# A hybrid encoder block on one core: the last gate half in seven products, and q and k computed among three gate halves

## The chip, the cores and the metric

The kernel runs on one core of one Trainium2 chip. The metric is the device time of one execution in microseconds; of several runs the median is taken. The core's engines work side by side and each takes its own instructions in order: TensorE (PE: matmuls, with PEld for its weight loads), VectorE (DVE), ScalarE (ACT), GpSimd (POOL) and SyncE (SP). DMAs are issued by SP, ACT and POOL and carried by 16 DMA engines.

## What is computed

One layer over 256 tokens of width 2048, all in float32:

```python
xn = rms_norm(x, norm_pre_w[l])
z = xn @ w_in[l]
u_lru, g_lru, q, k, v, g_attn, m_lru, m_attn = jnp.split(z, split_at, axis=-1)
u = centred_depthwise_conv(u_lru, conv_w[l], conv_b[l])
h = (rg_lru(u, ..., False) + rg_lru(u, ..., True))
y_a = h.astype(x.dtype) * jax.nn.silu(g_lru)
q = partial_rope(q.reshape(bsz, s, N_HEADS, HEAD_DIM), cos, sin)
k = partial_rope(k.reshape(bsz, s, N_KV_HEADS, HEAD_DIM), cos, sin)
y_b = windowed_gqa(q, k, v, attn_sink[l]) * jax.nn.silu(g_attn)
merged = (jax.nn.sigmoid(m_lru) * (y_a @ w_proj_a[l])
          + jax.nn.sigmoid(m_attn) * (y_b @ w_proj_b[l]))
x = x + rms_norm(merged @ w_out[l], norm_post_w[l])
```

There are 16 heads of 128 columns in four groups, each group with its own k and v. The rotation (`partial_rope`) touches the first 32 columns of each head. The gates m_lru and m_attn have 2048 columns each.

## The kernel before

**Number format.** Every float32 operand of a matmul is split into a high part (a cast, on ACT) and a low part (the difference, on DVE), and a product is taken as three matmuls: high by high, high by low, low by high (`mm3`, L221). Activations are split once, weights as they arrive.

**Steps.** The program is a list of steps, written out by hand as words in `START`, `MERGE` and `OUT` (L55 to L66). One step is 1 MB of weights, in two halves. A letter names the product, a number its column block, the digit behind the dot its part along the contraction:

- `u`, `w`: the LRU's input; `g`, `h`: its silu gate and that of attention; `v`, `k`, `q`: attention; `p`, `b`: the two projections; `a`: the gate m_attn; `o`: the output product.
- Steps of g, h, w, k and q ("blk", `add_pair`, L227) hold weights as the stationary operand and take 8 matmuls of 512 and 8 of 256 columns a half. Steps of v, p, a, b and o ("quad", `add_rows`, L257) hold activations and take 12 matmuls of 512 columns a half.
- `Lm1.0` and the like ("part", class `Seven`, L338): half a gate (1024 columns) by Strassen's scheme, seven products m1 to m7 in place of eight, each in two parts of 12 matmuls. L and M are the two halves of m_lru, A the second half of m_attn, O half of the output product. The first half of m_attn is eight plain quads, a0 and a1. The sums of weights that m3 to m7 need are made by accumulating DMAs from POOL into "x" and "y" cells (`load`, L185). The sums of x are made once (`x_sums`, L327), kept in DRAM and loaded again for each gate half (`x_sum`, L333).

**Time in the program.** A half of a blk or quad and a whole part are one half step ("tick", L157). The loop at L1095 goes through the steps. At each half it issues the loads of the steps three to five ahead (`fetch`, L199), then the work that is due at this half step, then the cast for four halves ahead and the subtraction for three halves ahead (`split`, L207), then the matmuls. Work is put at a half step with `at`, or a number of half steps from now with `soon` (L160, L172); an engine's queue is filled in this order. Raw weights have a ring of three buffers; everything else lives in 45 units of 4 KB a partition. What does not fit is written to DRAM by `park` (L782) and fetched by `back` (L789), both on SP's queue, on which the raw loads are too.

**Order around the change.** Before, the gate halves L and M are woven into the steps of g, h, w and k. Then come q0, p0, q1, p1, q2, p2, q3, p3, then a0 and a1 woven with A, then b with the rest of A and the start of O, then the output.

**Attention.** `add_heads` (L804) takes a group's two column pairs from PSUM: `evac` (L809) scales them and `rotate` (L817) turns each pair's first 32 rows with operations on 32 partitions by 512, then splits them. `heads` (L916) puts the four heads of a group behind its q: the first head's scores five half steps later (`HEAD0`), the next ones every four (`STRIDE`). A head (L846) takes scores at its half step b, the masked maximum on DVE at b + 1, the exponentials on ACT at b + 2, the scale by the sum (L878) at b + 4, the transposes on PE (`flip`, L880) at b + 5, the split of the transposed at b + 6; a pair of heads is multiplied with v at b + 10. `yb_parts` (L911) splits the gated result for b. `gates`' sigmoids are taken by `gate_evac` (plain, L749) or `gate_sum` (seven products, L758); `gated_out` (L745) parks those of m_lru.

Of the kernel before, what the change touches and what calls it, by code (L numbers as in the profile page):

```python
# [15 lines left out]
F32 = mybir.dt.float32  # L16
# [13 lines left out]
UNITS = 45  # L30
DECAY = 12
SPIN = 10
HEAD0 = 5
STRIDE = 4
FIRST = 8
ROWS = 10
U0, GL0, Q0, K0, V0, GA0, ML0, MA0 = 0, 2048, 4096, 6144, 6656, 7168, 9216, 11264

# [13 lines left out]

MERGE = """q0.0 q0.1 q0.2 q0.3 p0.0 p0.1 p0.2 p0.3 q1.0 q1.1 q1.2 q1.3 p1.0 p1.1 p1.2 p1.3  # L55
    q2.0 q2.1 q2.2 q2.3 p2.0 p2.1 p2.2 p2.3 q3.0 q3.1 q3.2 q3.3 p3.0 p3.1 p3.2 p3.3
    a0.0 a0.1 Am1.0 a0.2 Am1.1 a0.3 Am2.0 a1.0 Am2.1 a1.1 Am5.0 a1.2 Am5.1 a1.3 b0.0 Am3.0 b0.1 Am3.1 b0.2 Am6.0
    b0.3 Am6.1 b1.0 b1.1 Am7.0 b1.2 Am7.1 b1.3 b2.0 Am4.0 b2.1 Am4.1 b2.2 b2.3 b3.0 Om1.0 b3.1 Om5.0 b3.2 b3.3""".split()
OUT = """o2.0 o2.1 Om1.1 o2.2 Om5.1 Om2.0 o2.3 Om3.0 Om6.0 Om3.1 o3.0 Om6.1 Om2.1 o3.1 Om7.0 Om7.1 Om4.0 Om4.1
    o3.2 o3.3""".split()  # L60

START = """u0.0 u0.1 u0.2 u0.3 v0.0 v0.1 v0.2 v0.3 g0.0 g0.1 h0.0 h0.1 w4.0 w4.1 g2.0 g2.1 h2.0 h2.1 w6.0 w6.1 g4.0 g4.1
    Lm1.0 h4.0 h4.1 Lm1.1 w8.0 Lm2.0 w8.1 Lm2.1 g6.0 Lm5.0 g6.1 h6.0 Lm5.1 h6.1 Lm3.0 w10.0 Lm3.1 w10.1 Lm6.0 g8.0
    g8.1 Lm6.1 h8.0 Lm7.0 h8.1 Lm7.1 w12.0 Lm4.0 w12.1 g10.0 Lm4.1 g10.1 Mm1.0 h10.0 Mm1.1 h10.1 Mm2.0 w14.0 w14.1
    Mm2.1 g12.0 Mm5.0 g12.1 Mm5.1 h12.0 Mm3.0 h12.1 g14.0 Mm3.1 g14.1 Mm6.0 h14.0 Mm6.1 h14.1 Mm7.0 k0.0 k0.1 Mm7.1
    k2.0 Mm4.0 k2.1 Mm4.1""".split()  # L66
XSUM = (18, 22, 26, 30, 34, 38, 42, 46)
LRU = (-4, 0, 2, 2, 2, 2, 2, 4)
QUADS = {"u": ("w_in", U0), "v": ("w_in", V0), "p": ("w_proj_a", 0), "a": ("w_in", MA0),
         "b": ("w_proj_b", 0), "o": ("w_out", 0)}  # L70
PAIRS = {"g": GL0, "h": GA0, "w": U0, "k": K0, "q": Q0}
SEVENS = {"L": ("w_in", ML0 + 1024), "M": ("w_in", ML0), "A": ("w_in", MA0 + 1024), "O": ("w_out", 0)}


PV_NORM = 0
# [38 lines left out]
def body(ctx, tc, x, xT, wall, wlru, pvec, npost, ident_d, mask_d, rope_d, out):  # L114
# [9 lines left out]
    def unit(name, dt=F32, shape=(P, 4, S)):  # L124
        return units.tile(list(shape), dt, tag="u", name=name)
# [7 lines left out]
    def half_unit(name, tag, dt=F32, bufs=2):  # L133
        return small.tile([P, 2, S], dt, tag=tag, name=name, bufs=bufs)
# [10 lines left out]
    def parts_of(h, l, src):  # L145
        nc.scalar.copy(h, src)  # L146
        soon(lambda: nc.vector.tensor_tensor(l, src, h.bitcast(F32), ALU.subtract))
# [24 lines left out]
    def soon(fn, d=1):  # L172
        at(now[0] + d, fn)
# [396 lines left out]
    def scaled(dst, ps, then=lambda: None, rows=True):  # L570
        def scale(src):
            nc.vector.tensor_tensor(dst, src, rbc.unsqueeze(1).to_broadcast([P, 2, S]), ALU.mult)
            then()

        def total():
            nc.vector.tensor_tensor(dst, ps[:, :, 0], dst, ALU.add)
            if rows:
                scale(dst)
            else:
                then()  # L580

# [161 lines left out]
        return gates[c]  # L743

    def gated_out(gates, c, t):  # L745
        if t == 1 and gates is tm:
            soon(lambda: park("tm", tm, c), 5)

    def gate_evac(gates, c):  # L749
        def done(t, ps):  # L750
# [7 lines left out]
    def gate_sum(gates, first=2):  # L758

        def done(t, c, ps, other, sign):  # L760
            to = gate_unit(gates, first + c)[:, t]

            def gate(src):
                nc.scalar.activation(to, src, AF.Sigmoid, scale=rtok[:, t:t + 1])
                gated_out(gates, first + c, t)

            if other is None:
                gate(ps)
            else:
                combine(to, ps, other, sign)  # L770
                soon(lambda: gate(to))
        return done

    Seven("L", xs, None, gate_sum(tm))
    Seven("M", xs, None, gate_sum(tm, 0))
    Seven("A", xs, None, gate_sum(sm))
    for n in range(8):
        behind(XSUM[n], lambda n=n: x_sums(n))
# [17 lines left out]

    def load_tables():
        t = unit("table")
        table.update(mask=t[:, 0:2], rope=t[0:ROT, 2:4])
        nc.sync.dma_start(table["mask"], mask_d)  # L800
        nc.sync.dma_start(table["rope"], rope_d)


    def add_heads(name, then):  # L804


        v = {}

        def evac(n):  # L809
            def done(ps):  # L810
                v[n] = half_unit(f"{name}f{n}", "uu")
                scaled(v[n], ps, rows=name == "k")
                for d in range(4):
                    soon(lambda d=d: rotate(n, d), d + 2)
            return done

        def rotate(n, d):  # L817
            t = v[n]
            r = t[0:ROT]
            if d == 0:  # L820
                v["s"] = small.tile([ROT, 2, S], F32, tag="upad", name=f"{name}s{n}", bufs=2)
                nc.vector.stream_shuffle(v["s"], r, swap)
                nc.vector.tensor_tensor(r, r, table["rope"][:, 0].unsqueeze(1).to_broadcast([ROT, 2, S]), ALU.mult)
            elif d == 1:
                s = v["s"]
                nc.vector.tensor_tensor(s, s, table["rope"][:, 1].unsqueeze(1).to_broadcast([ROT, 2, S]), ALU.mult)
                nc.vector.tensor_tensor(r, r, s, ALU.add)
            elif d == 2:
                if n == 0:
                    v["h"], v["l"] = unit(f"{name}h", F32R), unit(f"{name}l", F32R)  # L830
                parts_of(v["h"][:, n:n + 2], v["l"][:, n:n + 2], t)
            elif n == 2:
                then(v["h"], v["l"])
                v.clear()
# [11 lines left out]
    def head(hd, qh, ql, b, both):  # L846

        g, j = hd // 4, hd % 4
        sk = pv[:, PV_SINK + hd:PV_SINK + hd + 1]
# [48 lines left out]
        def gate_out():  # L898
            y = sga[g][:, j - 1:j + 1]
            nc.vector.tensor_tensor(y, both["o"], y, ALU.mult)  # L900
            both.clear()
            if j == 3 and g < 3:
# [13 lines left out]
    def heads(g):  # L916
        def then(h, l):
            b = now[0] + HEAD0
            soon(lambda: back("sga", sga, g, (P, 4, S)), HEAD0 + 4)
            for j in range(4):  # L920
                if j % 2 == 0:
                    both = {}
                head(4 * g + j, h, l, b + STRIDE * j, both)
        return then


    def add_pa(c):
# [44 lines left out]
        return tick  # L972

    seven = Seven("O", ms, msum, lambda *a: o_sum(*a))
    heads_k = add_heads("k", lambda h, l: kv.update(kh=h, kl=l))

    def add_q(c):
        pair = add_heads(f"q{c}", heads(c))
        for n in (0, 2):
            pair(n)  # L980

# [11 lines left out]
        "a": lambda: add_rows(f"ma{c}_", xs, gate_evac(sm, c)),  # L993
# [195 lines left out]
```

## Time and profile before

| | |
|---|---|
| median of 3 runs | 889.14 us (889.12 to 889.55) |
| the profiled execution | 889.43 us, of which span 887.1 us |
| granted TensorE clock | 0.998 |
| moved by DMA | 235.13 MB, mean 265 GB/s |

The span runs from the first to the last instruction in the profile of one execution; the rest of that execution's time lies around it. The profile's page gives busy shares by engine, the chain of work that ended last (followed back from the last instruction to whatever released it), and groups of instructions with their line, shapes, total and mean. Idle time of an engine that is not on the chain costs nothing by itself.

### The profile page before, as it was taken

To read this page: it belongs to the slowest core of one execution; us is meant where nothing else is said; L and a number is where in the kernel's file an instruction comes from. 1 tells how busy PE (TensorE), PEld (TensorE's weight loads), DVE (VectorE), ACT (ScalarE), POOL (GpSimd) and SP (SyncE) were. 2 spreads that over 40 slices of the span, in tenths; PEclk is the share of its full clock that TensorE was granted. 3 is DMA by queue.
4 is the path that set the end of the run, shared out by engine and by line. 5 is a ranking of instruction groups with operands and counts; after the bars stand their busy time and mean duration, and the time that the engine had idled before them with its cause. 6 is when DMAs were issued, how large, how long until landed. Compare 5 with 4: busy or idle time off the path is not lost.

```text
span 887.1 us, 12275 instructions
## 1 busy us (share of the span) xinstructions
PE 877.8 (99%) x4566; PEld 753.3 (85%) x4566; DVE 713.3 (80%) x974; ACT 610.4 (69%) x885; POOL 58.6 (7%) x88
## 2 busy tenths in 40 slices
PE   9999999999999999999999999999999999999996
PEld 8888888888888888888888888888888888888885
DVE  6999999798988788989987678586667776687776
ACT  7689687878788787989654556356687564555654
POOL 0000000011001011100000000000101100000200
PEclk9999999999999999999999999999999999999999
DMA  9757699999968999974957456558999997899962
GB/s 331 270 191 250 197 366 235 375 312 301 313 235 240 312 313 313 308 243 145 350 190 276 175 206 217 188 192 321 249 318 329 306 300 244 284 325 377 236 177 96
DMA packets 51419, 235.13 MB, mean 265 GB/s; under 512 B 5376, under 2 KB 10240, under 8 KB 35104
## 3 DMA queue, kind: packets, MB, share of 16 engines
q1 hardware_dynamic: 41568, 200.03, 61.2%
q0 software_dynamic: 9216, 33.56, 19.4%
q10 hardware_dynamic: 576, 0.76, 0.3%
q8 instruction: 36, 0.59, 0.3%
q14 instruction: 23, 0.19, 0.1%
HBM read 218.60 MB, written 15.73 MB: 264 GB/s over the span
## 4 chain that ended last, share of the span: by engine, by line
PE 97%; DMA 2%; DVE 0%; ACT 0%; DVEq 0%; issue 0%; ACTq 0%
PE q L250 7%; PE ga L250 7%; PE gl L250 7%; PE u L250 5%; PE ga L248 3%; PE gl L248 3%; PE q L248 3%; PE u L248 3%; PE k L250 2%; PE Am L225 1%; PE Am L223 1%; PE Lm L223 1%; PE Mm L223 1%; PE Lm L224 1%; PE Am L224 1%; PE Mm L224 1%
## 5 line engine op out<-in xcount | busy, mean ns | idle before, releaser
L219 DVE TENSOR_TENSOR wl<-raw,wh 128x1024 fp32r<-128x1024 f32 (+1 forms) x264 | 311.5, 1200 | 42.8 <-ACT wh L217 37.0
L217 ACT CAST wh<-raw 128x1024 fp32r<-128x1024 f32 (+1 forms) x263 | 264.1, 1036 | 43.3 <-DMA raw<-wall_dram 38.8
L250 PE MATMUL ga<-xs,wh 128*128 128x512 f32 x256 | 63.4, 391 | 0.0
L250 PE MATMUL gl<-xs,wh 128*128 128x512 f32 x256 | 63.2, 391 | 0.0
L250 PE MATMUL q<-xs,wh 128*128 128x512 f32 x256 | 62.8, 391 | 0.0
L250 PEld LDWEIGHTS gl<-xs,wh 128*128 128x128 f32 x256 | 47.0, 188 | 9.1
L250 PEld LDWEIGHTS ga<-xs,wh 128*128 128x128 f32 x256 | 46.8, 188 | 8.9
L250 PEld LDWEIGHTS q<-xs,wh 128*128 128x128 f32 x256 | 46.6, 188 | 8.8
L146 ACT CAST ph<-pt 128x512 fp32r<-128x512 f32 x16 | 9.4, 588 | 62.3 <-PE pt L884 62.2
L250 PE MATMUL u<-xs,wh 128*128 128x512 f32 x192 | 47.3, 391 | 0.0
L250 PEld LDWEIGHTS u<-xs,wh 128*128 128x128 f32 x192 | 35.2, 188 | 6.7
L248 PE MATMUL q<-xs,wl 128*128 128x256 f32 x256 | 34.4, 284 | 0.0
L248 PEld LDWEIGHTS ga<-xs,wl 128*128 128x128 f32 x256 | 33.1, 191 | 1.2
L248 PEld LDWEIGHTS q<-xs,wl 128*128 128x128 f32 x256 | 33.1, 191 | 1.3
L248 PEld LDWEIGHTS gl<-xs,wl 128*128 128x128 f32 x256 | 32.8, 191 | 1.2
L248 PE MATMUL ga<-xs,wl 128*128 128x256 f32 x256 | 33.9, 283 | 0.0
L248 PE MATMUL gl<-xs,wl 128*128 128x256 f32 x256 | 33.2, 283 | 0.0
L864 DVE CUSTOM_DVE_ANT_0 p<-sc,table,pv 128x256 f32<-128x256 f32 x32 | 16.1, 540 | 19.9 <-PE sc L225 19.9
L248 PEld LDWEIGHTS u<-xs,wl 128*128 128x128 f32 x192 | 24.6, 191 | 0.9
L248 PE MATMUL u<-xs,wl 128*128 128x256 f32 x192 | 24.9, 283 | 0.0
L645 DVE SCALAR_TENSOR_TENSOR uu<-upad,pv,uu 128x256 f32<-128x256 f32 x48 | 23.2, 483 | 1.7
L146 ACT CAST ms<-mt 128x512 fp32r<-128x512 f32 x8 | 4.7, 588 | 23.5 <-PE mt L950 23.5
(524 smaller groups left out, 2256.8 us busy)
## 6 DMA issues: line engine op xcount, KB each, us to landing
raw<-wall_dram SPq DMA_DIRECT2D x127, 1024.0 KB, 6.7
lraw<-wlru_dram SPq DMA_DIRECT2D x8, 512.0 KB, 8.9
away<-xx SPq DMA_DIRECT2D x8, 512.0 KB, 8.5
Lm<-away SPq DMA_DIRECT2D x8, 512.0 KB, 10.5
Mm<-away SPq DMA_DIRECT2D x8, 512.0 KB, 9.9
Am<-away SPq DMA_DIRECT2D x8, 512.0 KB, 10.4
raw<-wall_dram SPq DMA_DIRECT2D x8, 256.0 KB, 4.6
parksga<-sg SPq DMA_DIRECT2D x4, 512.0 KB, 9.5
```

The costliest lines, as they stand in the source:

```text
L146: nc.scalar.copy(h, src)
L217: cast(hs, raw)
L219: nc.vector.tensor_tensor(ls, raw, hs.bitcast(F32), ALU.subtract)
L223: nc.tensor.matmul(ps, wh, xh, start=start, stop=False, skip_group_check=more)
L224: nc.tensor.matmul(ps, wh, xl, start=False, stop=False, skip_group_check=more)
L225: nc.tensor.matmul(ps, wl, xh, start=False, stop=stop, skip_group_check=more)
L248: nc.tensor.matmul(ps[:, 1], wl[:, sl], a[:, 0], start=False, stop=False)
L250: nc.tensor.matmul(ps, wh[:, sl], a, start=k == 0, stop=k == KT - 1)
L645: nc.vector.scalar_tensor_tensor(u, up[:, j, tap:tap + S], cw[:, tap:tap + 1], u, ALU.mult, ALU.add)
L864: nc.vector.tensor_tensor_reduce(p[:, t], sc[:, t], table["mask"][:, t], rtok_sc[:, t:t + 1], sk, ALU.add, ALU.max, m[:, t:t + 1])
```

## The change

1. The first half of m_attn is taken by seven products too, as group N: 14 parts in place of the eight quads a0 and a1. Its sigmoids are parked in DRAM and come back at b0 and b1.
2. All of q is computed before p. M's second half is woven with q0, g14 and h14; N with k, q1, q2 and q3. q0's four heads are kept in DRAM until their heads start.
3. Heads no longer follow their own q. They stand at set half steps: the first 16 half steps before p0.0, then one every three, group after group. A group's q is split two half steps before its first scores. The results of groups 0 and 1 are parked; those of 2 and 3 are split for b where they lie.
4. The rotation is packed: ACT copies the 32 rows of four heads into one tile of 128 partitions by 256, DVE turns them all at once, ACT copies them back.
5. p now runs without q between, and A's parts are woven with p3 and b.

```diff
-HEAD0 = 5
-STRIDE = 4
+HEAD0 = -16
+STRIDE = 3
 FIRST = 8
+QAWAY = 10
+QPARK = (0,)
...
-MERGE = """q0.0 q0.1 q0.2 q0.3 p0.0 p0.1 p0.2 p0.3 q1.0 q1.1 q1.2 q1.3 p1.0 p1.1 p1.2 p1.3
-    q2.0 q2.1 q2.2 q2.3 p2.0 p2.1 p2.2 p2.3 q3.0 q3.1 q3.2 q3.3 p3.0 p3.1 p3.2 p3.3
-    a0.0 a0.1 Am1.0 a0.2 Am1.1 a0.3 Am2.0 a1.0 Am2.1 a1.1 Am5.0 a1.2 Am5.1 a1.3 b0.0 Am3.0 b0.1 Am3.1 b0.2 Am6.0
-    b0.3 Am6.1 b1.0 b1.1 Am7.0 b1.2 Am7.1 b1.3 b2.0 Am4.0 b2.1 Am4.1 b2.2 b2.3 b3.0 Om1.0 b3.1 Om5.0 b3.2 b3.3""".split()
+MERGE = """p0.0 p0.1 p0.2 p0.3 p1.0 p1.1 p1.2 p1.3 p2.0 p2.1 p2.2 p2.3 Am1.0 p3.0 p3.1 Am1.1 p3.2 Am2.0 p3.3 Am2.1 b0.0
+    Am5.0 b0.1 Am5.1 b0.2 Am3.0 b0.3 Am3.1 b1.0 b1.1 Am6.0 b1.2 Am6.1 b1.3 Am7.0 b2.0 Am7.1 b2.1 Am4.0 b2.2 Am4.1
+    b2.3 b3.0 Om1.0 b3.1 Om5.0 b3.2 b3.3""".split()
...
-    g8.1 Lm6.1 h8.0 Lm7.0 h8.1 Lm7.1 w12.0 Lm4.0 w12.1 g10.0 Lm4.1 g10.1 Mm1.0 h10.0 Mm1.1 h10.1 Mm2.0 w14.0 w14.1
-    Mm2.1 g12.0 Mm5.0 g12.1 Mm5.1 h12.0 Mm3.0 h12.1 g14.0 Mm3.1 g14.1 Mm6.0 h14.0 Mm6.1 h14.1 Mm7.0 k0.0 k0.1 Mm7.1
-    k2.0 Mm4.0 k2.1 Mm4.1""".split()
+    Lm6.1 g8.1 h8.0 Lm7.0 h8.1 Lm7.1 w12.0 Lm4.0 w12.1 Lm4.1 g10.0 Mm1.0 g10.1 h10.0 Mm1.1 h10.1 Mm2.0 w14.0 Mm2.1
+    w14.1 Mm5.0 g12.0 Mm5.1 g12.1 h12.0 Mm3.0 h12.1 Mm3.1 q0.0 Mm6.0 q0.1 Mm6.1 q0.2 q0.3 Mm7.0 g14.0 Mm7.1 g14.1
+    Mm4.0 h14.0 Mm4.1 h14.1 Nm1.0 k0.0 k0.1 Nm1.1 k2.0 Nm2.0 k2.1 Nm2.1 q1.0 Nm5.0 q1.1 Nm5.1 q1.2 q1.3 Nm3.0 q2.0
+    Nm3.1 q2.1 Nm6.0 q2.2 Nm6.1 q2.3 Nm7.0 q3.0 q3.1 Nm7.1 q3.2 Nm4.0 q3.3 Nm4.1""".split()
...
-        if t == 1 and gates is tm:
-            soon(lambda: park("tm", tm, c), 5)
+        if t == 1 and (gates is tm or c < 2):
+            soon(lambda: park("tm" if gates is tm else "sm", gates, c), 5)
...
+    Seven("N", xs, None, gate_sum(sm, 0))
...
+                if n == 0:
+                    v["f"] = unit(f"{name}f")
+                scaled(v["f"][:, n:n + 2], ps, rows=name == "k")
+                soon(lambda: pack(n), 2)
+                if n == 2:
+                    for d, fn in enumerate((rotate, turned, unpack)):
+                        soon(fn, d + 3)
+                    soon(lambda: then(v["f"]), QAWAY if name in [f"q{c}" for c in QPARK] else 6)
...
+        def pack(n):
+            if n == 0:
+                v["r"] = small.tile([P, 2, S], F32, tag="upad", name=f"{name}r", bufs=2)
+            for j in (n, n + 1):
+                nc.scalar.copy(v["r"][j * ROT:(j + 1) * ROT, 0], v["f"][0:ROT, j])
+        def rotate():
+            r, s = v["r"][:, 0], v["r"][:, 1]
+            nc.vector.stream_shuffle(s, r, swap)
+            nc.vector.tensor_tensor(r, r, table["rope"][:, 0], ALU.mult)
+            nc.vector.tensor_tensor(s, s, table["rope"][:, 1], ALU.mult)
+        def turned():
+            nc.vector.tensor_tensor(v["r"][:, 0], v["r"][:, 0], v["r"][:, 1], ALU.add)
+        def unpack():
+            for j in range(4):
+                nc.scalar.copy(v["f"][0:ROT, j], v["r"][j * ROT:(j + 1) * ROT, 0])
...
+            if g > 1:
+                at(max(b + 12, end + hd // 2 - 6), lambda: yb_parts(hd // 2))
...
+    def heads(g, b, end):
+        def start():
+            h, l = unit(f"qh{g}", F32R), unit(f"ql{g}", F32R)
+            parts_of(h, l, qs.pop(g))
+            soon(lambda: back("sga", sga, g, (P, 4, S)), 6)
             for j in range(4):
                 if j % 2 == 0:
                     both = {}
-                head(4 * g + j, h, l, b + STRIDE * j, both)
-        return then
+                head(4 * g + j, h, l, b + STRIDE * j, both, end)
+        if g in QPARK:
+            at(b - 8, lambda: back("q", qs, g, (P, 4, S)))
+        at(b - 2, start)
...
+        if c < 2:
+            at(tick[f"b{c}.0"], lambda c=c: back("sm", sm, c))
+        heads(c, tick["p0.0"] + HEAD0 + 4 * STRIDE * c, tick["b0.0"])
```

More of the change, by code (lines that the diff above doesn't have):

```diff
@@ L63 @@
     Lm1.0 h4.0 h4.1 Lm1.1 w8.0 Lm2.0 w8.1 Lm2.1 g6.0 Lm5.0 g6.1 h6.0 Lm5.1 h6.1 Lm3.0 w10.0 Lm3.1 w10.1 Lm6.0 g8.0
-    g8.1 Lm6.1 h8.0 Lm7.0 h8.1 Lm7.1 w12.0 Lm4.0 w12.1 g10.0 Lm4.1 g10.1 Mm1.0 h10.0 Mm1.1 h10.1 Mm2.0 w14.0 w14.1
-    Mm2.1 g12.0 Mm5.0 g12.1 Mm5.1 h12.0 Mm3.0 h12.1 g14.0 Mm3.1 g14.1 Mm6.0 h14.0 Mm6.1 h14.1 Mm7.0 k0.0 k0.1 Mm7.1
-    k2.0 Mm4.0 k2.1 Mm4.1""".split()
+    Lm6.1 g8.1 h8.0 Lm7.0 h8.1 Lm7.1 w12.0 Lm4.0 w12.1 Lm4.1 g10.0 Mm1.0 g10.1 h10.0 Mm1.1 h10.1 Mm2.0 w14.0 Mm2.1
+    w14.1 Mm5.0 g12.0 Mm5.1 g12.1 h12.0 Mm3.0 h12.1 Mm3.1 q0.0 Mm6.0 q0.1 Mm6.1 q0.2 q0.3 Mm7.0 g14.0 Mm7.1 g14.1
+    Mm4.0 h14.0 Mm4.1 h14.1 Nm1.0 k0.0 k0.1 Nm1.1 k2.0 Nm2.0 k2.1 Nm2.1 q1.0 Nm5.0 q1.1 Nm5.1 q1.2 q1.3 Nm3.0 q2.0
+    Nm3.1 q2.1 Nm6.0 q2.2 Nm6.1 q2.3 Nm7.0 q3.0 q3.1 Nm7.1 q3.2 Nm4.0 q3.3 Nm4.1""".split()
 XSUM = (18, 22, 26, 30, 34, 38, 42, 46)
 LRU = (-4, 0, 2, 2, 2, 2, 2, 4)
-QUADS = {"u": ("w_in", U0), "v": ("w_in", V0), "p": ("w_proj_a", 0), "a": ("w_in", MA0),
+QUADS = {"u": ("w_in", U0), "v": ("w_in", V0), "p": ("w_proj_a", 0),
          "b": ("w_proj_b", 0), "o": ("w_out", 0)}
 PAIRS = {"g": GL0, "h": GA0, "w": U0, "k": K0, "q": Q0}
-SEVENS = {"L": ("w_in", ML0 + 1024), "M": ("w_in", ML0), "A": ("w_in", MA0 + 1024), "O": ("w_out", 0)}
+SEVENS = {"L": ("w_in", ML0 + 1024), "M": ("w_in", ML0), "N": ("w_in", MA0), "A": ("w_in", MA0 + 1024), "O": ("w_out", 0)}
 PV_NORM = 0
@@ L798, in load_tables @@
         t = unit("table")
-        table.update(mask=t[:, 0:2], rope=t[0:ROT, 2:4])
+        table.update(mask=t[:, 0:2], rope=t[:, 2:4])
         nc.sync.dma_start(table["mask"], mask_d)
@@ L810, in done @@
             def done(ps):
[L811 to L814, printed above, removed]
-            return done
[L817 to L834, printed above, removed]
+                if n == 0:
+                    v["f"] = unit(f"{name}f")
@@ L844, in v_evac, with head @@
         soon(lambda: nc.vector.scalar_tensor_tensor(vl, ps, rtok[:, t:t + 1], vh.bitcast(F32), ALU.mult, ALU.subtract))
-    def head(hd, qh, ql, b, both):
+    def head(hd, qh, ql, b, both, end):
         g, j = hd // 4, hd % 4
@@ L901, in gate_out @@
             both.clear()
-            if j == 3 and g < 3:
+            if j == 3 and g < 2:
                 soon(lambda: park("yb", sga, g), 4)
@@ L914, in yb_parts @@
         parts_of(yb[q][:, :, 0], yb[q][:, :, 1], sga[q // 2][:, n:n + 2])
[L916 to L919, printed above, removed]
+    def heads(g, b, end):
[3 more added lines that the diff above has]
+            soon(lambda: back("sga", sga, g, (P, 4, S)), 6)
             for j in range(4):
@@ L974, in body, with k_parts @@
     seven = Seven("O", ms, msum, lambda *a: o_sum(*a))
-    heads_k = add_heads("k", lambda h, l: kv.update(kh=h, kl=l))
+    def k_parts(f):
+        kv.update(kh=unit("kh", F32R), kl=unit("kl", F32R))
+        parts_of(kv["kh"], kv["kl"], f)
+    heads_k = add_heads("k", k_parts)
+    qs = {}
     def add_q(c):
-        pair = add_heads(f"q{c}", heads(c))
+        pair = add_heads(f"q{c}", lambda f: [qs.update({c: f}), c in QPARK and park("q", qs, c)])
         for n in (0, 2):
@@ L992, in body @@
         "p": lambda: add_pa(c),
-        "a": lambda: add_rows(f"ma{c}_", xs, gate_evac(sm, c)),
         "b": lambda: add_pb(c),
@@ L997, in body @@
         lru_pair(2 * c, tick[f"g{2 * c}.0"] + LRU[c])
-    at(tick["k0.0"] - 6, load_tables)
+    at(tick["q0.0"] - 6, load_tables)
     for c in range(4):
@@ L1004, in body @@
             at(tick["p0.0"] - 8 + 2 * c, lambda c=c: back("ya", sgl, c, (P, 4, S)))
+        if c < 2:
             at(tick["b0.0"] - 12 + 3 * c, lambda c=c: back("yb", sga, c, (P, 4, S)))
@@ L1008, in body @@
             at(tick["p0.0"] - 3 + n, lambda n=n: y_parts(n))
-        at(tick["b0.0"] - 6 + 3 * n // 2, lambda n=n: yb_parts(n))
+        if n < 4:
+            at(tick["b0.0"] - 6 + n, lambda n=n: yb_parts(n))
     npt, xr, yw = [], [[], []], [[], []]
@@ L1145, in tables @@
     c, s = np.cos(ang), np.sin(ang)
-    rope = np.stack([np.concatenate([c, c]), np.concatenate([-s, s])], axis=1).astype(np.float32)
+    rope = np.stack([np.concatenate([c, c] * (P // ROT)), np.concatenate([-s, s] * (P // ROT))], axis=1).astype(np.float32)
     return np.eye(P, dtype=np.float32), np.ascontiguousarray(mask), np.ascontiguousarray(rope)
```

## The prediction

> **What bounds the kernel now.** I read the page first (busy shares, the chain of waits), then one output tile on TensorE, then all waits, then windows, then groups by shape. "DMA share" in a window is the mean busy share of the 16 DMA engines.
>
> ```profile
> span 887.1 us, 12275 instructions
> PE 877.8 (99%) x4566; PEld 753.3 (85%) x4566; DVE 713.3 (80%) x974; ACT 610.4 (69%) x885; POOL 58.6 (7%) x88
> PE 97%; DMA 2%; DVE 0%; ACT 0%; DVEq 0%; issue 0%; ACTq 0%
> ```
>
> TensorE (PE) is the chain of work, bar the first loads. But a busy PE row can hide slow matmuls, so I take the rate from one output tile, p0's, whose 96 matmuls of 512 columns run back to back:
>
> ```profile
> L223 PE MATMUL pa__4419<-wh,ya x32: 389/389/389, 440.6 to 461.7; 128*128 128x512 f32 x32
> ```
>
> The 32 first products start at 440.6 to 461.7: 31 intervals of three matmuls in 21.1 us, so 21.1 / 93 = 0.227 us from start to start (389 ns is the pipelined length). A matmul of 256 columns takes 1.91 / 16 = 0.12 us by the chain in order of time:
>
> ```profile
> 53.67 1.91 PE gl L248 x16
> ```
>
> Then who makes PE wait, in the view of waits, and SP's own:
>
> ```profile
> ACT ph L146 <- PE pt L884: 62.2, 14, 5.5
> DVE wl L219 <- ACT wh L217: 59.5, 41, 4.6
> ACT wh L217 <- DMA raw<-wall_dram: 38.8, 20, 5.6
> PEld mt L950 <- DVE mg L939: 1.4, 4, 0.4
> PEld u_ps L540 <- DVE xs L471: 1.2, 1, 1.2
> ...
> SPq L205 <- DVE wl L219: 547.5, 111, 14.9
> ```
>
> Past the opening, PE waited 1.4 us for anyone (four times, the transposes L950). ACT waits for PE and for loads, DVE waits for ACT, and SP's weight loads wait 547.5 us for DVE to free a buffer: the loads stand ready, the buffers do not. All of it is hidden, so matmuls taken away are time taken away until a feeder gets too slow. How near the feeders come:
>
> ```profile
> 180.00:205.00 25.00, 25.00 (x145) 22.08 (x144) 24.11 (x31) 18.25 (x28) 4.49 (x7) 1.00 1.04 316
> 205.00:230.00 25.00, 25.00 (x139) 21.81 (x138) 21.08 (x25) 22.27 (x29) 4.36 (x5) 1.00 1.04 305
> 345.00:395.00 50.00, 50.00 (x284) 43.99 (x283) 44.48 (x54) 44.51 (x65) 5.23 (x6) 1.00 0.97 310
> 440.00:640.00 200.00, 200.00 (x1038) 171.08 (x1037) 144.59 (x246) 109.03 (x195) 3.48 (x4) 1.00 0.66 225
> 680.00:780.00 100.00, 99.99 (x449) 82.09 (x449) 70.88 (x85) 54.85 (x70) 10.42 (x12) 1.00 0.91 290
> ```
>
> Columns: PE, weight loads, DVE, ACT, POOL busy, granted clock, DMA share, GB/s. DVE at 24.11 of 25, ACT at 44.51 of 50 and DMA at 1.04 each left PE full. The stage of q and p (440 to 640) has DVE at 72%, ACT at 55%, DMA at 0.66: the change moves work into that gap.
>
> **The matmuls taken away.** A quad is 24 matmuls of 512 columns, a part 12. Last gate, first half: 8 quads (a0, a1) = 192 matmuls become 14 parts (N) = 168. k, q, p, b, o, heads and transposes keep their number. 24 x 0.227 = 5.45 us.
>
> The Trainium skill bears on this price (TensorE: Matmul & The Clock Gate, section "Back-to-back issue gap"): it gives 131 ns a matmul of 512 columns as the sustained rate of a real stream, by which the 24 would be worth an estimated 3.1 us. The row above shows 227 ns in a full stream, so the row decides.
>
> **What is added, and its cover.** Durations:
>
> ```profile
> L219 DVE TENSOR_TENSOR wl<-raw,wh 128x1024 fp32r<-128x1024 f32 x256 | 306.0, 1216 | 42.1 <-ACT wh L217 36.4 <-PE o L224 3.0 <-PE pb__6613 L225 1.1
> L217 ACT CAST wh<-raw 128x1024 fp32r<-128x1024 f32 x256 | 259.8, 1048 | 42.8 <-DMA raw<-wall_dram 38.3 <-PE Am L225 1.8 <-PE o L225 1.6
> L870 ACT ACTIVATE p<-p,nm 128x256 f32<-128x256 f32 x32 | 16.0, 504 | 4.2 <-DVE nm L865 4.2
> L870 ACT ACTIVATION_READ_ACCUMULATOR p<-p,nm 128x1 f32 x32 | 6.1, 189 | 0.0
> L878 ACT ACTIVATE p<-p,rd 128x256 f32<-128x256 f32 x32 | 14.5, 502 | 7.5 <-DVE rd L877 7.5
> L871 ACT ACTIVATE es<-nm,pv 128x2 f32<-128x2 f32 x12 | 3.4, 283 | 0.0
> L146 ACT CAST ph<-pt 128x512 fp32r<-128x512 f32 x16 | 9.4, 588 | 62.3 <-PE pt L884 62.2
> L764 ACT ACTIVATE mg<-mg,rtok 128x512 f32<-128x512 f32 x9 | 6.5, 727 | 4.1 <-DVE mg L756 4.1
> L680 ACT ACT_TABLE_LOAD x8 | 10.3, 1283 | 0.1
> L680 ACT ACTIVATE th<-gr,cpos 128x256 f32<-128x256 f32 x32 | 13.8, 515 | 0.0
> L523 ACT ACTIVATE diag<-diag 128x128 f32<-128x128 f32 x2 | 0.6, 312 | 4.4 <-DVE diag L522 4.4
> L310 DVE TENSOR_TENSOR xa<-xa 128x256 f32<-128x256 f32 x8 | 3.4, 425 | 0.3
> L822 DVE STREAM_SHUFFLE q1s<-q1f 32x512 f32<-32x512 f32 x2 | 1.5, 730 | 0.0
> L827 DVE TENSOR_TENSOR q3f<-q3f,q3s 32x512 f32<-32x512 f32 x2 | 1.4, 680 | 0.1
> ```
>
> Weights: 28 half parts replace 16 half quads, so 12 more casts (259.8 / 256 = 1.01 us, 12 us of ACT) and 12 more subtractions (306.0 / 256 = 1.20 us, 14 us of DVE). Rotation: 10 shuffles (0.73) and 30 products and sums on 32x512 (0.68) go, 28 us of DVE; 5 shuffles and 15 operations on 128x256 come, between 0.425 and 0.73 each, so 8.5 to 15 us. DVE thus gains nothing to speak of: 14 - 28 + 8.5 to 15, about zero. ACT also gets 40 copies of 32x256 (pack and unpack). No row has that shape; bounds are 0.31 (128x128) and 0.50 (128x256) each, 12 to 20 us, and I take 0.45 as a row's length follows its columns: 18 us. With two more table loads (2.6) ACT rises by some 33 us to 643, still 73% of the span.
>
> The dense place is where heads, N's last parts and p's start overlap. From the weights of Nm6.1 to those of p1.1, PE has 88.1 us of matmuls (the program's counts at 0.227 and 0.12). ACT there issues 32 weight casts (32), 30 passes over p and 16 reads of sums (15 + 3), 16 small copies (7), 7 table loads (9), 6 casts each of p and ya (7), 6 evacuations and gates (4), two casts of q (2), 8 small ones (2): 82 us, 93%, less what neighbours overlap (1.01 a cast against 1.048 alone). The window 345 to 395 had 89% and no wait of PE. So I cost it at nothing; uncovered, what comes late is a scale (L878) ahead of its transpose on PE. The last LRU pair, with its table loads, ends well before p instead of in p0, for g14.0 now stands 57 half steps ahead of p0.0, not 31.
>
> A rule of the skill speaks against this place: ScalarE: Activation LUTs (section "What ACT_TABLE_LOAD costs") puts a drain of about 1380 ns behind each 1283 ns load; seven would be an estimated 9.7 us more. In the rows, 8 of the 32 L680 operations follow a load directly and all 32 waited 0.0 us together, so by the trace the drain isn't there.
>
> **New waits.** Once per q group, four times, the low part of q is made one half step before its scores; before, it was five ahead. The nearest row is the transposes' wait of L950 on a DVE result of the half step before, 1.4 us in four. Bounds 0 to 1.4 us; I take 0.5, for DVE in p's stage is emptier. Behind these scores on PE's queue stand all weights' matmuls. q0's return from DRAM is a new wait on ACT with every later cast behind it; it is issued six half steps (16 us) ahead, and the like transfer lands in half that (below).
>
> **Transfers.**
>
> ```profile
> q1 hardware_dynamic: 41568, 200.03, 61.2%
> q0 software_dynamic: 9216, 33.56, 19.4%
> raw<-wall_dram SPq DMA_DIRECT2D x127, 1024.0 KB, 6.7
> sga<-parksga SPq DMA_DIRECT2D x4, 512.0 KB, 7.9
> Ax0a<-wall_dram POOLq DMA_DIRECT2D x3, 512.0 KB, 9.6
> ```
>
> N brings 8 sums of x, 8 plain and 16 accumulating half loads, for 6 fewer raw loads; the parked pieces net four more (two sm out and back; q once out and back for one yb). SP gets 14 more issues, POOL 16. Cost by the rows: 61.2% of 887.1 / 200.03 = 2.71 us/MB plain, 19.4% of 887.1 / 33.56 = 5.13 accumulating. The parts of m5 move in among b: the steps b0.0 to b2.0 (9 quads, 7 parts, 68.1 us of PE) now need 17.8 MB plain (11 weights of 1.05, 7 sums and 5 returns of 0.52) and 5.2 accumulating: 48.3 + 26.9 = 75 us of DMA in 68, share 1.10, above the plateau of 1.04. Prefetch hides that: a raw load is issued once the buffer of three steps before is free, three steps of 4.1 us on average (5.45 and 2.72 in turn), 12 us, before use, against 6.7 to land. I cost it at nothing.
>
> **Sum.** The profiled execution took 889.43 us (span 887.1 and 2.3 around it): 889.43 - 5.45 + 0.5 = 884.5. The median shown, 889.14, is 0.29 lower: 884.2.
>
> **The rivals.**
> - *ACT becomes the bound* between Nm6.1 and p1.1. For it: 93%, seven loads, heads every three half steps instead of four. Against: 89% hid fully, and ACT's lead over PE shows as its waits for pt (62.2 us in 14). If the copies cost 0.9 each, ACT has 89 us for 88, and its first half is denser by some 2 us: 3 us lost, 887.
> - *The DMA engines become the bound in b* (the one that ends slower). At 1.04 the windows moved as little as 305 GB/s; the 23.0 MB of b0.0 to b2.0 then take 75.5 us for 68.1, 7.4 us late, and the chain goes raw, cast, PE: 889.14 - 5.45 + 7.4 = 891.1. It decides once the lag eats the 12 us of lead less 6.7 to land; 7.4 is past that 5.3, and I price it whole because the parts of b2 and b3 follow with no slack stage. Against: SP waits for buffers 547.5 us.
> - *The change doesn't save what it says*: if the shorter parts leave PE waiting for weights as long as the matmuls took (each part needs two casts and two subtractions in 2.72 us), 889. Against: L and M run so at 96% DVE.
> - *The skill's matmul rate* (above): 889.14 - 24 x 0.131 + 0.5 = 886.5; the 227 ns row excludes it almost wholly.
>
> **Chances.** Forecast with under 1.5 us of loss (883.2 to 885.5) 0.70; ACT 0.12; DMA 0.09; no saving 0.07; the page's rate 0.02. The range 883.0 to 888.0 leaves out DMA and no saving. A measurement tells 0.2%, 1.8 us, from no change. Faster by more (under 887.4): the forecast, the page's rate and most of ACT's, 0.82; within: no saving and the rest, 0.09; slower (over 890.9): DMA, 0.09.
>
> **What would show it.** PE busy down 5 to 6 us and still one chain; matmuls 24 fewer; ACT near 643, DVE near 713; some 13 more MB moved. Wrong: waits of PE for p (L878's line) between Nm6.1 and p1.1 (ACT), for wh or wl in b with DMA share at 1.04 for over 70 us (DMA), for ql (the new hand-over).

## The result and the profile after

| | before | after |
|---|---|---|
| median of 10 runs each | 889.39 us | 893.60 us |
| after / before, 95% interval | | 1.0052 [1.0042, 1.0062] |
| span of the profiled execution | 887.1 us | 891.3 us |
| granted TensorE clock | 0.998 | 0.993 |
| moved by DMA | 235.13 MB | 247.94 MB |

The changed kernel is slower by half a per cent, 4.2 us by the medians; the forecast was 5 us faster. The page after, its engine row, its DMA queues and its chain of waits:

```profile
span 891.3 us, 12379 instructions
PE 875.4 (98%) x4542; PEld 750.4 (84%) x4542; DVE 711.4 (80%) x959; ACT 643.2 (72%) x937; POOL 72.5 (8%) x104
q1 hardware_dynamic: 43680, 204.42, 61.9%
q0 software_dynamic: 11520, 41.95, 24.3%
PE 90%; DMA 5%; issue 4%; DVE 1%; POOLq 0%; ACT 0%; ACTq 0%; POOL 0%; DVEq 0%
raw<-wall_dram SPq DMA_DIRECT2D x121, 1024.0 KB, 7.5
```

The work is what the diff said: 24 matmuls fewer, and less PE time. But the chain, which was 97% PE, is 90% PE now, and DMA has 5% of it, `raw<-wall_dram` above all. The view of waits of PE shows where:

```profile
PE mt L963 <- DVE sm L952: 6.5, 2, 5.6
PE Am L225 <- DMA Am<-away: 0.7, 1, 0.7
```

and the windows of the two kernels over the same 100 us place it (columns as in the prediction). First the kernel before, then the kernel after:

```profile
640.00:680.00 40.00, 40.00 (x189) 33.34 (x188) 28.91 (x44) 33.43 (x50) 3.49 (x4) 1.00 0.98 316
680.00:715.00 35.00, 35.00 (x156) 28.96 (x156) 20.69 (x21) 20.58 (x24) 6.96 (x8) 1.00 1.04 317
715.00:740.00 25.00, 25.00 (x115) 20.47 (x114) 20.60 (x27) 14.29 (x19) 1.06 (x2) 1.00 0.79 276
```

```profile
440.00:640.00 200.00, 200.00 (x1048) 171.42 (x1047) 150.42 (x250) 151.44 (x254) 12.19 (x14) 1.00 0.83 276
640.00:680.00 40.00, 40.00 (x187) 33.17 (x186) 31.73 (x47) 28.51 (x45) 3.55 (x5) 1.00 0.89 282
680.00:715.00 35.00, 27.84 (x120) 22.36 (x119) 16.70 (x18) 11.40 (x13) 5.13 (x6) 0.96 1.05 302
714.00:719.00 5.00, 5.00 (x15) 3.99 (x14) 4.89 (x8) 4.18 (x6) 0.00 (x0) 0.53 1.01 417
```

Until 680 us PE is full in both. In 680 to 715, within b0 and before b1.0, PE after stands idle for 35.00 - 27.84 = 7.2 us, with the DMA share at 1.05 and DVE and ACT idle for half the time and more (16.70 and 11.40 us busy): they wait too. Then the clock drops: in 714 to 719 the granted clock is 0.53, and 15 matmuls are done where full speed does 22. The chain of waits after, in order of time, from the load to the first matmuls behind the stall (start, duration, what):

```profile
681.98 26.52 DMA raw<-wall_dram
...
708.60 1.05 ACT wh L219
...
709.68 1.23 DVE wl L221
710.90 0.61 DVE sm L951
...
712.86 0.70 DVE sm L952
...
713.61 0.90 PE mt L963 x3
714.52 0.43 PE pb__6909 L225
...
718.36 0.43 PE pb__6909 L225
718.78 0.28 PE pb__6909 L226
719.06 0.23 PE pb__6909 L227
```

One raw load takes 26.52 us. ACT's cast waits 8.02 us for it, as its row in the timeline of ACT has it:

```profile
708.60 1.99 ACT L219 CAST wh<-raw 128x1024 fp32r<-128x1024 f32 x2 [8.02 <-DMA raw<-wall_dram]
```

DVE's subtraction waits for the cast; behind that subtraction on DVE's queue stands the merge of b0 (L951, L952), and PE's transposes of b0 wait for the merge. PE's own timeline:

```profile
712.28 0.47 PE L963 MATMUL mt<-ident,sm 128*128 128x128 f32 x1 [5.64 <-DVE sm L952]
```

PE had ended its last matmul before that at 712.28 - 5.64 = 706.6, so the merge could have begun at least 3 us ahead of the subtraction at 709.68. Ten matmuls then run at 0.43 us instead of 0.23, 2 us more. So -5.45 (matmuls) + 7.2 (idle) + 2.0 (half clock) = 3.7 of the 4.2 us by which the span grew; transposes at half clock are among the rest.

Why the load took so long: the DMA view of the stretch 680 to 715, before and then after (packets, MB, share of 16 engines; then the median us to landing of the raw loads issued in it):

```profile
q1 hardware_dynamic: 1477, 7.57, 54.1%
q0 software_dynamic: 965, 3.49, 50.1%
raw<-wall_dram SPq DMA_DIRECT2D x4, 1024.0 KB, 15.3
```

```profile
q0 software_dynamic: 1094, 3.96, 56.6%
q1 hardware_dynamic: 1262, 6.59, 47.7%
raw<-wall_dram SPq DMA_DIRECT2D x4, 1024.0 KB, 24.4
```

q0 carries POOL's accumulating loads, q1 SP's plain ones. The engines are full in both. After, q0 took 0.47 MB more in the same 35 us, and q1 got 0.98 MB less; since a MB on q0 takes 35 x 56.6% / 3.96 = 5.0 us of the engines and one on q1 35 x 47.7% / 6.59 = 2.5, that is the exchange one expects, two for one. In the time of the late load alone, 682 to 708.5, the two queues had nearly the same number of packets through:

```profile
q0 software_dynamic: 877, 3.17, 60.0%
q1 hardware_dynamic: 884, 4.62, 44.6%
```

POOL issues an accumulating load as soon as its cell is free, not when its sum is due. Its queue in time, after (the last column is the idle time before, and what ended it):

```profile
672.99 0.89 POOL L192 DMA_DIRECT2D Ax0a<-wall_dram  x1 [28.09 <-DVE wl L221]
675.92 0.87 POOL L192 DMA_DIRECT2D Ax0b<-wall_dram  x1 [2.04 <-DVE wl L221]
679.93 0.86 POOL L192 DMA_DIRECT2D Ax1a<-wall_dram  x1 [3.14 <-DVE wl L221]
...
702.25 0.86 POOL L192 DMA_DIRECT2D Ay1b<-wall_dram  x1 [2.95 <-DVE wl L221]
```

Eight such loads (m6, then m7) go out between 673 and 702; Ax0b, issued at 675.92, is cast at 717.1, over 40 us later. The Trainium skill has the rule for this (DMA: Bandwidth & Descriptors, section "Queues, rings and completion order"): each DMA engine takes turns between the queues that have work, a packet at a time. The packets of 682 to 708.5, 877 against 884, agree with it: while q0 has work, the raw loads get their turn, not the whole engine, and what SP issued earlier stands ahead of them.

### The profile page after: what moved, and what is told of

It is laid out like the page before. It is cut to its first block, busy times and chain, and to the rows that moved or that the text cites. A ratio compares the mean times of both kernels' runs of the same rounds, so it can differ in the third digit from the quotient of the medians.

```text
span 891.3 us, 12379 instructions
## 1 busy us (share of the span) xinstructions
PE 875.4 (98%) x4542; PEld 750.4 (84%) x4542; DVE 711.4 (80%) x959; ACT 643.2 (72%) x937; POOL 72.5 (8%) x104
## 2 busy tenths in 40 slices
DMA packets 55838, 247.94 MB, mean 278 GB/s; under 512 B 5856, under 2 KB 10720, under 8 KB 40288
## 4 chain that ended last, share of the span: by engine, by line
PE 90%; DMA 5%; issue 4%; DVE 1%; POOLq 0%; ACT 0%; ACTq 0%; POOL 0%; DVEq 0%
PE ga L252 7%; PE gl L252 7%; PE q L252 7%; PE u L252 5%; DMA raw<-wall_dram 4%; PE ga L250 3%; PE gl L250 3%; PE q L250 3%; PE u L250 3%; PE k L252 2%; PE Nm L225 1%; PE Nm L226 1%; PE Lm L225 1%; PE Mm L225 1%; PE Mm L226 1%
## 5 line engine op out<-in xcount | busy, mean ns | idle before, releaser
L221 DVE TENSOR_TENSOR wl<-raw,wh 128x1024 fp32r<-128x1024 f32 (+1 forms) x252 | 299.3, 1203 | 73.0 <-ACT wh L219 62.6
L219 ACT CAST wh<-raw 128x1024 fp32r<-128x1024 f32 (+1 forms) x251 | 253.8, 1036 | 56.3 <-DMA raw<-wall_dram 49.1
L877 ACT ACTIVATE p<-p,nm 128x256 f32<-128x256 f32 x32 | 16.0, 502 | 8.5 <-DVE nm L872 8.5
## 6 DMA issues: line engine op xcount, KB each, us to landing
Lm<-away SPq DMA_DIRECT2D x8, 512.0 KB, 13.3
```

The lines of the kernel that those rows point to most:

```text
L219: cast(hs, raw)
L221: nc.vector.tensor_tensor(ls, raw, hs.bitcast(F32), ALU.subtract)
L877: nc.scalar.activation(p[:, t], p[:, t], AF.Exp, bias=nm[:, t:t + 1], accum_out=dn[:, t:t + 1])
```

## The experiments

Theory D: the burst of accumulating loads delays the raw loads of b1.0, and the rest follows. The first four runs try it and its rivals. All ratios are against the kernel before.

**e1, hold the loads back.** GpSimd reads a column of the weights of the current step before it issues an accumulating load of A, so the load does not go out before DVE has split the weights of the step five ahead of its part. There are eight such reads, for the sixteen accumulating loads of A.

```diff
             if lead == 5 and m in (("m5", "m6", "m7", "m4") if self.sums is None else ("m6", "m7", "m4")):
+                if self.name == "A":
+                    nc.gpsimd.tensor_copy(pace, parts[2 * len_now[0]][1][:, 0:1].bitcast(F32))
                 load(self.cell(m, q), p, True)
...
             if h == 0:
+                len_now[0] = i
                 for lead in (3, 4, 5):
```

> The changed kernel with each accumulating load of group A held on POOL until DVE has split the weights of the step five ahead of the use (a 1-column copy on POOL that reads that low part). Nothing is left out. Theory D (in b0 the accumulating loads go out as soon as their cells are free, far ahead of need, share the DMA engines with the urgent raw load of b1.0 and make it land 23 to 26 us after its issue): the raw load of b1.0 lands within 14 us, PE's wait at the transposes before b1.0 goes from 5.8 us to under 1.5, and the time is 884 to 886. Rival O (the order on DVE's queue, the merge of b0 behind a subtraction, makes the wait): no change of more than 3 us, 890 to 894. Rival S (the return of the parked gate sm from DRAM makes the raw load late): as O.

Measured: 883.97 us, 0.9939 [0.9922, 0.9955]. The first accumulating load of m6 leaves at 687.48 instead of 672.99, and PE is full. The window of e1, and its DMA view over the same stretch:

```profile
680.00:715.00 35.00, 35.00 (x159) 28.75 (x158) 24.27 (x29) 16.83 (x21) 6.97 (x9) 1.00 1.03 328
```

```profile
q1 hardware_dynamic: 1737, 8.88, 64.9%
q0 software_dynamic: 703, 2.58, 37.7%
```

At nearly the same share the engines moved 2.29 MB more on the plain queue. The waits added on GpSimd are worth 9.6 us by the medians, and this kernel is faster than both.

**e2, the order on DVE.** The transposes of b0 to b2 one half step later, so that they stand behind other matmuls on PE.

```diff
-                    soon(lambda i=i: turn(i), 1 + i * (1 if c == 3 else 2))
+                    soon(lambda i=i: turn(i), (1 if c == 3 else 2) + i * (1 if c == 3 else 2))
```

> The changed kernel with the first pair of transposes after each of b0, b1, b2 one half step later (and the second pair with it), so that PE takes the first half of the next b step before it needs DVE's merge. Nothing is left out. Theory D alone: the raw load lands as late as before, PE then waits for the weights of b1.0 instead: from 706.5 to 709.7 us for the cast and 710.9 for the low part, so 3 to 4.5 us in place of 7, and less half clock: 888 to 890. Rival O (order is the whole cause): the wait goes to under 1 us, 884 to 885.5.

Measured: 890.79 us, 1.0016 [1.0006, 1.0027], 0.8 above the upper end of what D gave and 5.3 above the upper end of what the order on DVE alone (rival O) gave. The merge behind the subtraction costs about 3 us; the load stays late, and PE waits for the weights themselves:

```profile
PE pb__6899 L225 <- ACT wh L219: 3.1, 1, 3.1
PE pb__6899 L226 <- DVE wl L221: 0.8, 1, 0.8
```

**e3, the returns of the parked gate.** sm0 comes back ten half steps earlier, sm1 three half steps behind b1's start.

```diff
         if c < 2:
-            at(tick[f"b{c}.0"], lambda c=c: back("sm", sm, c))
+            at(tick["b0.0"] + (-10, 15)[c], lambda c=c: back("sm", sm, c))
```

> The changed kernel with the returns of the parked gate sm moved out of the crowded half steps: sm0 ten half steps earlier (in p3), sm1 three half steps later than b1.0. Nothing is left out. Rival S: 884 to 886. Theory D: 1 MB of some 23 MB is moved, 1.3 us of the 9.7 lost comes back, 891 to 893.5. Rival O: no change, 893 to 894.

Measured: 893.03 us, 1.0046 [1.0030, 1.0062], with the same waits as the changed kernel (6.5 us for L952, 0.9 for Am). The place of these returns is not the cause (rival S gave 884 to 886); between D and O this run does not decide.

**e4, leave accumulating loads out.** Those of A's m7 are left out (m_attn's second half differs by it).

```diff
-                load(self.cell(m, q), p, True)
+                if (self.name, m) != ("A", "m7"):
+                    load(self.cell(m, q), p, True)
```

> The changed kernel without the four accumulating half loads of A's product m7 (the weights of m7 are then those of m3 alone, so half of the gate m_attn is computed otherwise); 2.1 MB and some 11 us of DMA engine time less in b0. Theory D: the raw load of b1.0 lands in time, PE's wait at the transposes is under 2 us, 883.5 to 886. Rivals O and S: 890 to 894.

Measured: 884.42 us, 0.9947 [0.9932, 0.9962]. No stall. The matmuls are all there, so what is missing is DMA work alone. With e1, D's cause is shown from two sides: later, or fewer, accumulating loads, and the stall is gone.

What of the change made the burst? The other runs take its parts one by one.

**e5, the parts of A spread over p again.** m1, m2 and m5 among p2 and p3, so that m5 leaves b, and b woven as before.

```diff
-MERGE = """... p2.2 p2.3 Am1.0 p3.0 p3.1 Am1.1 p3.2 Am2.0 p3.3 Am2.1 b0.0
-    Am5.0 b0.1 Am5.1 b0.2 Am3.0 b0.3 Am3.1 b1.0 b1.1 Am6.0 ...
+MERGE = """... p2.2 Am1.0 p2.3 Am1.1 p3.0 Am2.0 p3.1 Am2.1 p3.2 Am5.0 p3.3 Am5.1 b0.0
+    Am3.0 b0.1 Am3.1 b0.2 Am6.0 b0.3 Am6.1 b1.0 b1.1 Am7.0 ...
```

> The changed kernel with the parts of A put back among p's last quads as densely as they stood among the old a quads (m1, m2 and m5 spread over p2.2 to p3.3, b0.0 to b2.2 woven as before), so that m5's two parts leave b and m6's and m7's accumulating loads go out when b has fewer plain loads. Theory D (the burst of accumulating loads beside dense plain loads makes a raw load of b late): no wait of PE over 1.5 us in b, 884 to 887 us. Rival P (the returns of the parked sm and q pieces alone overload b, wherever the parts of A stand): the stall stays, 891 to 895 us. A stall of another place, as p now holds more parts, is open: up to 2 us.

Measured: 890.06 us, 1.0005 [0.9995, 1.0016]: between the two. Less of a stall (3.4 us of waits in b, with slow matmuls behind), not none; neither statement holds.

**e6, the control.** The holding back of e1 in the kernel before.

> The kernel before, with the same holding back of group A's accumulating loads as in e1 (GpSimd reads one column of the weights five steps ahead of the part before it issues them). Theory D: before had no stall in b to take away, so 888.7 to 889.9 us. Rival H (holding back accumulating loads is worth 5 us or more by itself, by less traffic at a time or a higher clock, stall or no stall): 884 to 886 us.

Measured: 889.07 us, 1.0003 [0.9993, 1.0012]. Pacing is worth nothing where there is no stall, so e1's gain is the stall's.

**e7, m5 among b0 in the kernel before**, with m3, m6, m7 and m4 behind it as in the changed kernel.

```diff
-    ... a1.1 Am5.0 a1.2 Am5.1 a1.3 b0.0 Am3.0 b0.1 Am3.1 b0.2 Am6.0
+    ... a1.1 a1.2 a1.3 b0.0 Am5.0 b0.1 Am5.1 b0.2 Am3.0 b0.3 Am3.1
```

> The kernel before, with only the place of m5's two parts changed: out of the a quads, among b0, with m3, m6, m7 and m4 behind them as in the changed kernel (a quads, q and p untouched, nothing parked that was not). Theory D: the same work with the same matmuls now stalls in b as the changed kernel does; 4 to 10 us more than before, 893 to 899 us, PE's transposes waiting for DVE and ACT's cast for raw. Rival P (the extra returns of parked pieces do it): no stall, 889 to 890 us.

Measured: 888.94 us, 0.9997 [0.9987, 1.0007], PE full in 680 to 715. This half of my theory falls: moving m5 into b does not make the stall.

**e8, one plain transfer less.** The changed kernel without the parking of p3's product, which SP writes at 673.63, ahead of b1.0's loads (b3 reads p2's product instead, so the output differs).

```diff
-                soon(lambda: park("pa", tm, c), 4)
+                if c < 3:
+                    soon(lambda: park("pa", tm, c), 4)
+                else:
+                    parked["pa", 3], tm[3] = parked["pa", 2], None
```

> The changed kernel without the parking of p3's product (0.5 MB written at 673.6 in the trace after, ahead of b1.0's raw loads on SP's queue; b3 then reads p2's product, so that its output differs). Theory D2 (the two queues take turns packet by packet, so that each 0.5 MB in rows of 4 KB that stands ahead of a raw load delays it by 3.8 to 3.9 us while accumulating loads are outstanding; what the change put there, this write above all, uses up the lead that the kernel before and e7_am5 still had): b1.0's raw lands some 4 us earlier, PE waits 2 to 5 us in b instead of 8.6, 886.5 to 890.5 us. Rival P0 (a single transfer more or less doesn't matter, only the parts' order does): 892.5 to 894.5 us.

Measured: 888.16 us, 0.9989 [0.9976, 1.0001]: 5.4 us off for half a MB. The raw load issued at 682.10 lands after 21.8 us instead of 26.5, PE waits 2.3 us, and the clock stays at 1.00. D2 gave this (886.5 to 890.5 us, some 4 us of landing). The trace is of an execution of 886.20 us; the ten range from 885.92 to 890.88, with a mean granted clock of 0.993 to 0.998, so the half clock is spared in this execution, and not shown to be in all.

**e9, those transfers in the kernel before.** e7 with three writes of 0.5 MB added, where the changed kernel brings sm0 back, parks p3's product and brings sm1 back.

```diff
+    def extra(n):
+        d = dram.tile([P, 1024], F32, name=f"extra{n}")
+        nc.sync.dma_start(d, xs[0].rearrange("p a b c -> p (a b c)").bitcast(F32))
+
+    for n, hs in enumerate((tick["b0.0"], tick["b0.0"] + 3, tick["b1.0"])):
+        at(hs, lambda n=n: extra(n))
```

> The kernel e7_am5 (before, with m5's parts among b0) with three writes of 0.5 MB to DRAM added, of x's first parts, read by nobody: at b0.0, three half steps later and at b1.0, where the changed kernel brings sm0 back, parks p3's product and brings sm1 back. Theory D2: with the order and the plain bytes of the changed kernel its stall comes too, 891 to 899 us, with b's raw loads landing in over 18 us. Rival O (the stall needs something else that the changed kernel has, the emptier lead of DVE and ACT or the weights' steps): no stall, 888.5 to 890 us.

Measured: 889.18 us, 1.0001 [0.9992, 1.0011]: no stall, D2 fails here as a sufficient cause. Something else of the change is needed. The POOL queue of this kernel, in time, shows one difference:

```profile
673.86 0.86 POOL L190 DMA_DIRECT2D Ax0a<-wall_dram  x1 [41.12 <-DVE wl L219]
674.99 0.89 POOL L190 DMA_DIRECT2D Ax0b<-wall_dram  x1 [0.27 <-issue]
685.77 0.88 POOL L190 DMA_DIRECT2D Ax1a<-wall_dram  x1 [9.90 <-DVE wl L219]
...
706.15 0.86 POOL L190 DMA_DIRECT2D Ay1b<-wall_dram  x1 [3.49 <-issue]
```

The second pair of m6 leaves 6 us later than in the changed kernel (685.77 against 679.93), for the subtraction that frees its cell comes later. ACT and DVE still have heads to do in this stretch: the last gating of a head is at 690.96 on DVE, in the changed kernel at 681.27. Hence theory D3: with the heads out of the way, the feeders run ahead of PE, and cells come free early.

**e10, the heads later** by four half steps, to put that last gating at about 691.

```diff
-HEAD0 = -16
+HEAD0 = -12
```

> The changed kernel with all heads four half steps later (HEAD0 -12 instead of -16), so that the last product of a head with its gate on DVE falls some 10 us later, to about 691 us, where the kernel before with m5 among b0 (e7_am5) has it; in the changed kernel it comes at 681.27. Theory D3 (the emptier queues of ACT and DVE let the weights' casts and subtractions run ahead, cells come free earlier, and GpSimd's accumulating loads of m6 and m7 go out without a gap from 673 to 714; heads among them hold them back): gaps between the accumulating loads, raw loads of b1.0 landing in 12 to 18 us, PE waits under 3 us in b, 884 to 888 us. Rival B (the heads' place does nothing for the burst, or their work among b only adds to the queue that is late): 892 to 897 us.

Measured: 890.29 us, 1.0018 [1.0002, 1.0034]: 3.3 us off, between D3's range and its rival's. The trace is of an execution of 893.68 us, one of three over 893 among the ten (the others: 887.78 to 891.15); in it the accumulating loads are little fewer (3.83 MB against 3.96), the raw loads land sooner (20.2 us against 24.4), and PE still waits 3.6 us. Nor did the run set what it was meant to set. The last two products of heads with their gate, in time:

```profile
678.76 0.69 DVE L907 TENSOR_TENSOR sga<-o,sga 128x512 f32<-128x512 f32 x1
698.79 0.68 DVE L907 TENSOR_TENSOR sga<-o,sga 128x512 f32<-128x512 f32 x1
```

The last comes at 698.79, not at 691, so work of heads now stands among b0's, as the rival has it. The heads' place has a share in the time; D3 is neither shown nor refuted.

**e11, e1 and e2 together.**

> e1_pace and e2_turn together: the accumulating loads of group A held back, and the transposes of b0 to b2 one half step later. In e1_pace PE still waited 0.7 us for b's transposes and 0.7 us for one weight. If the waits were additive and independent: 883.2 to 884.0 us. If the later transposes only move the same wait to the next cast (as e2_turn alone has its remaining waits at weights): 883.7 to 884.7 us, no different from e1_pace's 883.97.

Measured: 883.84 us, 0.9946 [0.9929, 0.9962], not to be told from e1.

The stretch 680 to 715 over these runs, each number from its window or DMA view (accumulating MB is q0's, plain MB q1's, raw the median to landing of the raw loads issued in it, idle 35 us less PE's busy time; all of these are of the one profiled execution, whose time stands beside the median):

| kernel | accumulating MB | plain MB | raw, us | PE idle, us | this execution, us | median, us |
|---|---|---|---|---|---|---|
| e3 | 4.00 | 6.48 | 26.8 | 7.4 | 893.28 | 893.03 |
| after | 3.96 | 6.59 | 24.4 | 7.2 | 893.12 | 893.60 |
| e2 | 4.08 | 6.35 | 23.8 | 3.9 | 889.27 | 890.79 |
| e8 | 4.04 | 6.39 | 21.7 | 2.3 | 886.20 | 888.16 |
| e10 | 3.83 | 6.86 | 20.2 | 3.6 | 893.68 | 890.29 |
| e5 | 3.40 | 7.78 | 20.1 | 2.1 | 889.91 | 890.06 |
| before | 3.49 | 7.57 | 15.3 | 0.0 | 889.43 | 889.39 |
| e9 | 3.36 | 7.69 | 14.6 | 0.0 | 890.41 | 889.18 |
| e7 | 3.42 | 7.51 | 13.5 | 0.0 | 888.79 | 888.94 |
| e6 | 3.18 | 7.09 | 13.3 | 0.0 | 889.08 | 889.07 |
| e1 | 2.58 | 8.88 | 12.0 | 0.0 | 884.16 | 883.97 |
| e4 | 1.86 | 9.76 | 11.5 | 0.2 | 884.16 | 884.42 |
| e11 | 2.54 | 8.96 | 9.7 | 0.0 | 883.74 | 883.84 |

In these traces PE hardly stands where raw loads land within some 15 us, and stands where they take 20 or more. The accumulating MB alone don't order the rows: e5 has fewer than before and lands later; its steps in this stretch are others. Holding these loads back or leaving some out (e1, e4) is the one change that takes the whole stall away; what SP has ahead (e8), the parts' order (e5) and the heads' place (e10) are worth 3.3 to 5.4 us each by the medians. So that the burst makes the loads late is shown; what in the change makes the burst hurt is not. No run undid two of these together, so which pair suffices is open.

## Why the prediction was wrong

**The step that failed** is the one headed "Transfers", at its last sentences: "Prefetch hides that: a raw load is issued once the buffer of three steps before is free [...] 12 us, before use, against 6.7 to land. I cost it at nothing." The lead was not the mistake: the load issued at 681.98 was waited for from 708.60 - 8.02 = 700.6 on, so it had 18.6 us, more than the 12. The landing was. 6.7 us is the median of 127 loads of the whole program; in this very stretch the trace of before gives 15.3 (the DMA view above), which the prediction did not ask for, and the changed kernel 26.5. Costed at nothing, it measured 9.6 us: after's 893.60 against 883.97 of e1, which has the same matmuls and transfers and one thing else: eight short reads on GpSimd, which set when A's accumulating loads go out.

**The demand was counted right and then dismissed.** 75 us of DMA for 68 of PE, and a lag of 7.4 us for 5.3 of slack, stood in the text. Against it I set "SP waits for buffers 547.5 us", a total over the program that says nothing of this stretch. The row of 680 to 715 after shows the DMA share at 1.05 while PE idles.

**The rival that came true** is "The DMA engines become the bound in b": 891.1 us at 0.09, against 893.60. Its place, its plateau and its first link, raw to cast, are right. Two things it did not have: on DVE's queue the merge of b0 stands behind the late subtraction, so PE stalls at the transposes (e2: some 3 us), and the idle time is followed by half clock. On that the Trainium skill has a rule (TensorE: Matmul & The Clock Gate, section "Part 1: The HAM clock gate (the "warmup" mystery)"): about 3.4 us idle halve the clock, and as much busy time brings it back. The row of 0.53 behind a wait of 5.6 us agrees, and so does e8's trace, where the longest wait is 1.3 us and the clock 1.00; e5's does not (last section). Nor is the bound one of bytes: e1 moves the same 247.94 MB with no stall. It is a matter of when they are asked for. So it is in part luck that the rival's time, reckoned from bytes, came within 2.5 us of the measured one.

**The matmuls taken away** were right: 4566 to 4542, and with the stall gone e1 stands 5.4 us under before (4.0 to 6.9 by its interval), where 5.45 was forecast. That leaves no room for "The change doesn't save what it says" (889), nor for the 3.1 us of the rival on the matmul rate.

**"ACT becomes the bound"** did not come: PE is at 200.00 of 200.00 in 440 to 640, and its waits hold none for p. The busy time of ACT, forecast at some 643, is 643.2; two terms of that sum are off and offset each other. The copies, priced at 0.45 us, take 0.40, 16 us in all instead of 18, and the twelve casts more are worth 14.7 us by their rows instead of 12. DVE's 713 is 711.4, the 13 MB more are 12.8.

```profile
L841 ACT COPY q3f<-q3r 32x256 f32<-32x256 f32 x4 | 1.6, 406 | 0.2
```

**"New waits"**, put at 0.5 us, are 0: no row of PE's waits names ql or a score. Without it the sum of the forecast is 883.7, and e1 measures 883.97.

**The range**, 883.0 to 888.0, left out a case with a chance of 0.09, though the demand above the plateau was known and nothing read from that stretch spoke against it. It is the case that came.

## What to carry to other kernels

Where a stage needs more DMA time than it has compute, read how long its loads take to land in that stretch, not the median of the program, and set it against their lead. A transfer that may start as soon as its buffer is free takes the engines from one that is due sooner: hold it back by a small dependency on an engine with time to spare, and test that on the kernel before too, where it should do nothing. When a change relieves the engines that free buffers, ask whether transfers now start earlier and what they meet (here this is argued from the queues of e9 and the changed kernel, not shown).

## What was not expected of the hardware

Full DMA engines moved 302 GB/s with 3.96 MB of accumulating loads in 35 us and 333 GB/s, at 0.98, with 1.86 MB. An accumulated MB costs twice the engine time of a plain one, 5.0 against 2.5 us, so the share says "full" at either rate. A stall of 5.6 us cost 2.0 us more by the clock, ten matmuls at 0.43 us. Shorter waits can be followed by half clock too. In e5, in PE's timeline and the window of the 3 us behind it:

```profile
715.33 0.30 PE L963 MATMUL mt<-ident,sm 128*128 128x128 f32 x1 [0.97 <-issue]
716.61 0.84 PE L963 MATMUL mt<-ident,sm 128*128 128x128 f32 x3 [0.98 <-DVE sm L952]
717.00:720.00 3.00, 3.00 (x10) 2.42 (x9) 3.00 (x4) 3.00 (x6) 0.00 (x0) 0.50 1.03 309
```

Two waits of under 1 us each, close together, precede a clock of 0.50 here, while in e8 waits of 1.33 and 1.00 us leave it at 1.00. What decides between them is open.
